# One 384-column projection from unshifted tokens, with V moved by 64 rows by DMA

## The chip, the cores and the metric

The kernel runs on one core of one Trainium2 chip. The metric is the device time of one launch in microseconds (us). Times shown are medians of several runs, each of the whole kernel. Names of engines in the profile: PE is TensorE's matmul, PEld its weight load, DVE is VectorE, ACT is ScalarE, POOL is GpSimd, SP is SyncE, which in this kernel issues nearly all DMAs.

## The reference

One encoder block on x of shape (1, 2048, 1024). The input is normalized, projected, and goes through two attention mixers: A with a window of 128 and grouped keys, B with three groups of eight heads whose windows and dilations are (128, 1), (512, 4) and (2048, 16). Their gated outputs are merged, projected and added to x.

```python
h = rms_norm(x, norm_gain[layer])
proj = h @ w_in[layer]
qa, ka, va, qb, kb, vb, ga, gb, mg = jnp.split(proj, split_idx, axis=-1)
...
for g, (window, dilation) in enumerate(B_GROUPS):
    o, l = dilated_group(qb[:, :, g], kb[:, :, g], vb[:, :, g], window, dilation,
                         rel_bias[:, c0:c0 + B_HEADS_PER_GROUP])
...
alpha = jax.nn.softmax(jnp.stack(lses, axis=0), axis=0)
yb = jnp.sum(alpha[..., None].astype(x.dtype) * jnp.stack(outs, axis=0), axis=0)
yb = yb.reshape(bsz, S, B_WIDTH) * jax.nn.silu(gb)
...
x = x + merged @ w_out[layer]
```

For dilation d, the tokens of one residue class (every d-th token) form a sequence of their own of 2048 / d tokens, and each of its tokens sees the 64 neighbours on either side. Queries and keys are normalized per head, with a bias by distance.

## The kernel before

**Operands.** x is normalized, scaled and split into two half-precision parts, XH (the rounded value) and XL (the rest), kept on chip for the whole main phase as 8 chunks of 128 channels by 2048 tokens, with 256 columns behind them (SE = 2048 + 256). Weights are split the same way into wh and wl. A product in nearly full precision is three matmuls: XH by wh, XH by wl, XL by wh.

**Units.** The main phase runs over 14 units (list UNITS): two units of A (four query heads, one key head, one value head each) and twelve of B (head pair p from 0 to 3, group g from 0 to 2; two query, two key, two value heads). Each unit has 384 weight columns: for B 128 of queries, 128 of keys, 128 of values. A unit goes through the 2048 tokens in 16 blocks of 128 tokens of one residue class, named (r, c): class r, block c. A class has n blocks: 16 in group 0, 4 in group 1, 1 in group 2.

**Slots.** The planner runs over slots, one per pair of blocks, 8 per unit, 112 in all. In a slot the matmuls of the pair's projections are written into TensorE's stream one by one, and all other steps are put in a queue of due times (functions `at` and `until`) measured in slots, and written out when TensorE's stream has come to that place. Each engine works in the order in which its instructions were written out. The constants EVAC, NORM, LS, LAGS and LV are these due times.

**Projection.** `Pair.matmuls` writes 24 matmuls (8 channel chunks by 3 operand pairs) into one PSUM bank "pj" (two banks). The tokens are the stationary operand, the weights the moving one, so that the result has tokens on partitions. In A and in group 2, one matmul makes all 384 columns. In groups 0 and 1 (`un.shift`), the query columns are made from the block's own 128 tokens, and the key and value columns from 128 tokens that lie 64 earlier (`subset(..., aligned=False)`), in a second series of 24 matmuls. So a query block i needs the keys and values of just the two shifted blocks i and i + 1. The first shifted block wraps: it has the last 64 tokens of the sequence and the first 64, and for that GpSimd copies the first 256 tokens behind XH and XL (`x_again`).

**After a pair's projection.** ScalarE copies queries and keys out of PSUM (`evac_qk`) and V's rounded part (`v_hi`), VectorE makes V's rest (`v_lo`); V goes into a tile "vt" (10 buffers) or "vw" for the wrapped first block (4 buffers), beside a column with a constant for the softmax denominator. Then come square, statistics, a reciprocal square root on GpSimd, scaling, gain, the split into two parts, and `turn`: SP issues DMA transposes that put heads on partitions (tile "kq", 4 buffers; one per block in B, and one for both blocks in A). Within a block's part of kq, queries and keys follow one another, each 128 tokens wide. The wrapped first block of group 0 gets a tile of its own (kq0), since the last query block reads it too.

**Items.** An `Item` is a query block with two heads. `logits` multiplies queries and keys into PSUM (one key range per matmul; two neighbouring whole blocks of one pair as one of 256 columns through `un.both`), `maxima` adds the bias and takes row maxima on VectorE, `exps`, `hi` and `lo` make the probabilities in two parts, `turn` lets SP transpose them (tile "pt"), and `values` multiplies them by V, LV slots after the start of the item. Where an item has fewer keys than its blocks are wide, `room` fills the rest of the row with zeros, so the value products always use whole blocks of 128 rows.

**SP's queue** carries weight loads, key transposes, transposes of probabilities, stores and loads of the B groups' partial results ("zd"), and stores of sums of x for the last third ("sd"). It works through them in the order of their due times: what waits holds up what stands behind.

**Last third.** After the main phase the gates, branch projections and the output projection run. There `piece` makes weight sums, and uses the 256 columns behind XH and XL as the place from which it stores them (`place`, `store`).

Of the kernel before, what the change touches and what calls it, by code (L numbers as in the profile page):

```python
# [22 lines left out]
F16 = mybir.dt.float16  # L23
# [7 lines left out]
S = 2048  # L31
D = 1024
NT = S // 128
# [5 lines left out]
PSC = 2.0 ** 14  # L39
VSC = 2.0 ** -13  # L40
SX = 2.0 ** 9
SE = S + 256
NG = 12


# [63 lines left out]
X_GB = ((0, 1), (1, 4))  # L109
X_AG, H_AT = .9, (.1, .35)  # L110
XR_BUFS = 6
XT_BUFS = 2
KQ_BUFS = 4
VT_BUFS = 10
PT_BUFS = 4
N_BIAS_A = 384
N_BIAS_B = 256
# [2 lines left out]
def block_kernel(tc, x, xt, w_units, w_gate, w_mrg, w_out, w_bra, w_brk, gain, qkg, sink, bias_a, bias_b, b_merge, out):  # L120
# [29 lines left out]
    ones = cst.tile([128, 128], F32, name="ones")  # L150
    G.memset(ones[:], 1.0)

    XH = xp.tile([128, NCH, SE], F16, name="XH")
    XL = xp.tile([128, NCH, SE], F16, name="XL")
    gp2, gi2 = [], []

    def pow2(mx, name):
# [593 lines left out]
    class Unit:  # L751


        def __init__(self, u):
            self.kind, self.idx, self.g = UNITS[u]
            self.u = u
            assert ("w", u) in done
            self.wh, self.wl = wtiles[u][3:5]
            if self.kind == "A":
                self.nq, self.nk, self.nv = 4, 1, 1  # L760
                self.d, self.n = 1, NT
            else:
# [6 lines left out]
            self.both, self.apart = {}, set()  # L769
# [27 lines left out]
    def subset(X, g, r, c, aligned):  # L797
        o = 128 * c if aligned else (128 * c or S // DIL[g]) - 64
        return xclass((XH, XL)[X], g, r)[:, :, o:o + 128]

    class Pair:

# [6 lines left out]
        def matmuls(self, i):  # L809
            un, (r, c) = self.un, self.subsets[i]  # L810
            self.ps[i] = ps = pj_p.tile([128, 512], F32, name="pj")
            out = []
            for a, b, aligned in ((0, 128, True), (128, 384, False)) if un.shift else ((0, 384, True),):
                h, lo = subset(0, un.g, r, c, aligned), subset(1, un.g, r, c, aligned)
                k = 0
                for ch in range(NCH):
                    for lhs, rhs in ((h, un.wh), (h, un.wl), (lo, un.wh)):
                        out.append(lambda lhs=lhs, rhs=rhs, ch=ch, a=a, b=b, k=k: T.matmul(  # L818
                            ps[:, a:b], lhsT=lhs[:, ch, :], rhs=rhs[:, ch, a:b], start=(k == 0), stop=(k == 23)))
# [30 lines left out]

        def v_lo(self, i):
            vt, psv = self.vt[i]
            nv = self.un.nv
            V.scalar_tensor_tensor(vt[:, :nv, 66:130], psv, VSC, vt[:, :nv, 0:HD], OP.mult, OP.subtract)
            self.un.v[self.subsets[i]] = vt

        def square(self):
            n = 2 * self.nh * HD
# [41 lines left out]
                G.tensor_copy(sp[:, i, nh:, :, :], sp[:, i, nq:nh, ::-1, :])  # L900

        def turn(self):
            kq = wk.tile([128, 12, 128], F16, name="kq", bufs=KQ_BUFS)
            outs = [kq[:, 6 * i:6 * i + 6] for i in range(2)]
            if self.un.shift and self.un.n == NT and self.subsets[0][1] == 0:
                outs[0] = wk.tile([128, 6, 128], F16, name="kq0", bufs=1)[:]
                self.un.apart.add(self.subsets[0])
            if self.un.kind == "A":
                nc.sync.dma_start_transpose(out=kq[:], in_=self.sp[:].rearrange("p s a b c -> p (s a b c)"))
            for i, s in enumerate(self.subsets):  # L910
                if self.un.kind == "B":
                    nc.sync.dma_start_transpose(out=outs[i], in_=self.sp[:, i].rearrange("p a b c -> p (a b c)"))
                self.un.kq[s] = outs[i]
            if len({s[0] for s in self.subsets}) == 1 and self.subsets[0] not in self.un.apart:
                self.un.both[self.subsets[0]] = kq[:].rearrange("p (i a) b -> p a i b", i=2)


    class Item:
        def __init__(self, un, r, i, h0):
            self.un, self.r, self.i, self.h0 = un, r, i, h0  # L920
            n = un.n
            self.p0 = 0
            if un.kind == "A":
                cs = [c for c in (i - 1, i, i + 1) if 0 <= c < n]
                self.keys = [((0, c), 0, 128) for c in cs]
                self.b0 = 128 * (cs[0] - i + 1)
            elif n == 1:
# [31 lines left out]
        def logits(self):  # L959
            un = self.un  # L960
            q = un.kq[(self.r, self.i)]
            if un.kind == "A":
                self.sv = [s_p.tile([128, 512], F32, name="s")[:, :self.W] for _ in range(2)]
            else:
                t = s_p.tile([128, 512], F32, name="s")
                self.sv = [t[:, self.W * j:self.W * j + self.W] for j in range(2)]
            for j in range(2):
                h = self.h0 + j
                kh = 0 if un.kind == "A" else h
                o, keys = 0, list(self.keys)  # L970
                while keys:
                    s, k0, k1 = keys.pop(0)
                    kt, w = un.kq[s][:, :, k0:k1], k1 - k0
                    if w == 128 and s in un.both and keys and keys[0] == ((s[0], s[1] + 1), 0, 128):
                        keys.pop(0)
                        kt, w = un.both[s], 256
                    for v in range(2):
                        T.matmul(self.sv[j][:, o:o + w], lhsT=q[:, h, :],  # L978
                                 rhs=kt[:, un.nq + kh + v * un.nk], start=(v == 0), stop=(v == 1))
                    o += w  # L980
# [38 lines left out]
        def values(self):  # L1019
# [3 lines left out]
            for j in range(2):  # L1023
                vh = 0 if un.kind == "A" else j
                for k, (p, c0, w) in enumerate(((self.ph, 0, HD + 1), (self.ph, 66, HD), (self.pl, 0, HD + 1))):
                    for s, key in enumerate(self.segs):
                        T.matmul(self.po[:, j, :w], lhsT=p[:, n * j + s, :], rhs=un.v[key][:, vh, c0:c0 + w],  # L1027
                                 start=(k == 0 and s == 0), stop=(k == 2 and s == n - 1))

        def z_load(self):  # L1030
# [759 lines left out]
    def piece(n, due):  # L1790
# [20 lines left out]
            r.append(w_sums(*raw, lambda t: t[:], tile))  # L1811

        def place(x, i):
            return (XH, XL)[x][:, i, S:SE]

        def store(x, a, e):
            o = 512 * c + 256 * m
            d = (wbd[k, x].rearrange("p (i o) -> p i o", i=7)[:, a:e, o:o + 256] if j < 4
                 else wod[:, a:e, x, j - 4, 256 * m:256 * m + 256])
            nc.sync.dma_start(out=d, in_=(XH, XL)[x][:, a:e, S:SE])  # L1820

        def hi(i):
            A.activation(place(0, i), r[0][0][i], AF.Copy, scale=sc[:])
# [454 lines left out]
```

## Time and profile before

| | us |
|---|---|
| median of 3 runs | 1884.11 (1883.85 to 1885.31) |
| the profiled execution | 1884.2 |
| its span, first to last instruction | 1882.4 |
| TensorE busy, matmuls | 1865.5 |
| VectorE busy | 1485.5 |
| ScalarE busy | 1242.8 |
| GpSimd busy | 579.1 |

The main phase's projections run from 108.0 to 1201.9 us of the span; the last third follows. By line, 45% of the chain of waits that ended last are the projection matmuls of line 818. In a row of the profile, "x" gives a count, and a matmul's duration is from its issue to the modelled end of its last result; consecutive matmuls overlap, so that the distance between their starts, in the timeline, is what they cost when TensorE is the limit. "128x256" is the size of the result, 128 partitions by 256 columns; "<-wh,XL 128*128" names the two operands and the size of the stationary one.

### The profile page before, as it was taken

To read this page: it belongs to the slowest core of one execution; us is meant where nothing else is said; L and a number is where in the kernel's file an instruction comes from. 1 tells how busy PE (TensorE), PEld (TensorE's weight loads), DVE (VectorE), ACT (ScalarE), POOL (GpSimd) and SP (SyncE) were. 2 spreads that over 40 slices of the span, in tenths; PEclk is the share of its full clock that TensorE was granted. 3 is DMA by queue.
4 is the path that set the end of the run, shared out by engine and by line. 5 is a ranking of instruction groups with operands and counts; after the bars stand their busy time and mean duration, and the time that the engine had idled before them with its cause. 6 is when DMAs were issued, how large, how long until landed. Compare 5 with 4: busy or idle time off the path is not lost.

```text
span 1882.4 us, 50311 instructions
## 1 busy us (share of the span) xinstructions
PE 1865.5 (99%) x18802; PEld 1430.3 (76%) x18802; DVE 1485.5 (79%) x3806; ACT 1242.8 (66%) x3002; POOL 579.1 (31%) x1363
## 2 busy tenths in 40 slices
PE   8999999999999999999999999999999999999999
PEld 5457996788999899998999989744444446776775
DVE  6649967998788788878789888857788764977885
ACT  8538877987777777677777667647667865433441
POOL 0024343444355345544355443510000001232121
PEclk9999999999999999999999999999999999999999
DMA  9236979897797688886898867877779978854552
GB/s 360 101 101 142 180 167 168 164 204 167 143 182 162 143 171 165 178 164 147 171 168 157 164 134 149 159 238 262 213 235 266 275 226 286 274 163 121 147 147 71
DMA packets 650021, 340.33 MB, mean 181 GB/s; under 512 B 459952, under 2 KB 590896, under 8 KB 648368
## 3 DMA queue, kind: packets, MB, share of 16 engines
q1 hardware_dynamic: 649632, 336.86, 74.3%
q8 instruction: 147, 2.41, 0.6%
q14 instruction: 98, 0.80, 0.2%
q10 hardware_dynamic: 144, 0.26, 0.0%
HBM read 149.05 MB, written 77.86 MB: 121 GB/s over the span
## 4 chain that ended last, share of the span: by engine, by line
PE 94%; DMA 2%; ACT 1%; DVE 1%; issue 1%; POOL 0%; SPq 0%; DVEq 0%; ACTq 0%; POOLq 0%
PE pj L818 45%; PE fps L1726 16%; PE fps L2051 8%; PE fps L2136 8%; PE s L978 5%; PE pv L1027 5%; PE pj L373 2%; PE pj L314 2%; PE fps L314 1%; DMA pt<-p 1%; PE pt L1081 1%; DMA wraw<-in_w_units_dram 0%; DMA xq<-in_xt_dram 0%; DVE pr L993 0%; DMA gtd<-yo 0%
## 5 line engine op out<-in xcount | busy, mean ns | idle before, releaser
L818 PE MATMUL pj<-wl,XH 128*128 128x128 f16 (+2 forms) x2816 | 715.3, 268 | 0.0
L818 PE MATMUL pj<-wh,XL 128*128 128x128 f16 (+2 forms) x2816 | 711.5, 269 | 0.0
L818 PE MATMUL pj<-wh,XH 128*128 128x128 f16 (+2 forms) x2816 | 708.7, 268 | 0.0
L818 PEld LDWEIGHTS <-XH 128*128 128x128 f16 x5632 | 576.6, 112 | 55.0
L818 PEld LDWEIGHTS <-XL 128*128 128x128 f16 x2816 | 315.6, 112 | 24.2
L993 DVE CUSTOM_DVE_ANT_0 pr<-s,b,ubuf 128x256 f32<-128x256 f32 (+3 forms) x512 | 218.9, 465 | 41.0 <-PE s L978 38.1
L1010 DVE SCALAR_TENSOR_TENSOR p<-pr,p 128x512 f16<-128x512 f32 (+2 forms) x256 | 194.4, 759 | 53.2 <-ACT p L1006 49.5
L885 POOL TENSOR_TENSOR rw<-rw,g 128x128 f32<-128x128 f32 (+1 forms) x224 | 148.3, 682 | 192.5 <-DVE rw L878 178.8
L2061 POOL TENSOR_TENSOR g<-g,t 128x512 f32<-128x512 f32 x32 | 48.3, 1510 | 484.8 <-DVE t L1983 484.4
L1726 PEld LDWEIGHTS <-wh 128*128 128x128 f16 x952 | 93.1, 98 | 111.3 <-issue 1.3
L836 ACT ACTIVATE rw<-pj 128x256 f32<-128x256 f32 (+1 forms) x224 | 87.3, 390 | 131.6 <-PE pj L818 131.0
L900 POOL COPY spl<-spl 128x256 f16<-128x256 f16 (+1 forms) x224 | 97.7, 465 | 244.4 <-DVE spl L895 243.7
L1006 ACT ACTIVATE p<-pr 128x512 f16<-128x512 f32 (+2 forms) x256 | 157.6, 616 | 4.6 <-POOL zz L1135 0.4
L2051 PE MATMUL fps<-y,bigh 128*128 128x128 f16 x1792 | 153.4, 219 | 0.0
L2051 PE MATMUL fps<-y,bigl 128*128 128x128 f16 x896 | 151.7, 219 | 0.0
L978 PE MATMUL s<-kq 128*128 128x128 f16 (+2 forms) x1552 | 149.3, 232 | 1.0 <-DVE nmA L993 0.9
L2136 PE MATMUL fps<-WO,mf 128*128 128x512 f16 x660 | 147.5, 379 | 0.0
L2051 PEld LDWEIGHTS <-bigh 128*128 128x128 f16 x1792 | 139.0, 98 | 7.3
L978 PEld LDWEIGHTS <-kq 128*128 128x128 f16 x1584 | 118.0, 98 | 19.8 <-issue 1.8
L1027 PE MATMUL pv<-vt,pt 128*128 128x65 f16 (+1 forms) x2784 | 131.6, 193 | 0.8 <-DMA pt<-p 0.7
L1027 PEld LDWEIGHTS <-pt 128*128 128x128 f16 x3024 | 120.0, 97 | 14.8 <-DMA pt<-p 1.8
L891 ACT ACTIVATE spl<-rw 128x512 f16<-128x512 f32 (+1 forms) x112 | 72.1, 643 | 76.5 <-POOL vt L847 70.1
(282 smaller groups left out, 3767.2 us busy)
## 6 DMA issues: line engine op xcount, KB each, us to landing
wraw<-in_w_units_dram SPq DMA_DIRECT2D x56, 384.0 KB, 4.0
g<-mgd SPq DMA_DIRECT2D x64, 256.0 KB, 5.2
mgd<-t SPq DMA_DIRECT2D x43, 256.0 KB, 4.5
wraw<-in_w_mrg_dram SPq DMA_DIRECT2D x41, 256.0 KB, 5.1
zd<-z SPq DMA_DIRECT2D x128, 66.0 KB, 2.1
zz<-zd SPq DMA_DIRECT2D x64, 132.0 KB, 3.5
ytd<-yo SPq DMA_DIRECT2D x32, 256.0 KB, 3.6
sd<-so SPq DMA_DIRECT2D x32, 256.0 KB, 2.8
```

The lines of the kernel that those rows point to most:

```text
L818: out.append(lambda lhs=lhs, rhs=rhs, ch=ch, a=a, b=b, k=k: T.matmul(ps[:, a:b], lhsT=lhs[:, ch, :], rhs=rhs[:, ch, a:b], start=(k == 0), ...
L836: A.activation(self.rw[:, n * i:n * i + n], self.ps[i][:, :n], AF.Copy)
L885: G.tensor_tensor(q[:, i, :un.nq, :], q[:, i, :un.nq, :], g, OP.mult)
L900: G.tensor_copy(sp[:, i, nh:, :, :], sp[:, i, nq:nh, ::-1, :])
L978: T.matmul(self.sv[j][:, o:o + w], lhsT=q[:, h, :], rhs=kt[:, un.nq + kh + v * un.nk], start=(v == 0), stop=(v == 1))
L993: V.tensor_tensor_reduce(out=self.pv[:, j, self.p0:self.p0 + W], in0=self.sv[j], in1=un.bias[:, self.h0 + j, self.b0:self.b0 + W], scale=I ...
L1006: A.activation(self.sp[:, :128 * n], self.pr, AF.Copy, scale=PSC)
L1010: V.scalar_tensor_tensor(self.sp[:, 128 * n:], self.pr, PSC, self.sp[:, :128 * n], OP.mult, OP.subtract)
L1027: T.matmul(self.po[:, j, :w], lhsT=p[:, n * j + s, :], rhs=un.v[key][:, vh, c0:c0 + w], start=(k == 0 and s == 0), stop=(k == 2 and s == n ...
L1726: T.matmul(b[k][:], lhsT=w[:, i, ch, :], rhs=xform(PROD[i][0], lo, ch, q), start=(i < 3 and n == 0), stop=(n == 11), skip_group_check=True)
L2051: out.append(lambda p=p, c=c, wl=wl, yl=yl, n=n: T.matmul(ps[:, 128 * p:128 * p + 128], lhsT=w[wl][:, i, c, p, :], rhs=y[:, yl, c, :], sta ...
L2136: out.append(lambda p=p, ml=ml, wl=wl, k=k: T.matmul(ps[:], lhsT=m[:, ml, p, :], rhs=WO[:, i, wl, p, :], start=(fresh and k == 0), stop=(k ...
```

## The change

All units now project all 384 columns in one series of 24 matmuls from unshifted tokens. Nothing is copied behind XH and XL any more, and these have 2048 columns.

Keys stay in unshifted blocks. In B the two blocks of a pair are now laid out in kq such that each head's keys of the pair are 256 tokens in a row; a query block's key range (64 before to 64 after it) is cut at multiples of 256, so it is one range of 192 at an end, or two of 192 and 64 columns. The transposes stay one per block, and write blocks of 128 at a distance of 256. Group 0 has no key tile of its own for the first block.

V of all units lies in one ring "vr" of 20 places in place of the tiles vt and vw. Where nothing is shifted, V is written there directly. In groups 0 and 1 it is written to a tile "vs" (one per pair, 2 buffers), and SP moves it into the ring by DMA, shifted by 64 rows (`v_move`, due 0.68 slots after the pair's projection): the first half of block c into the second half of place c, the second half into the first half of place c + 1. A class with n blocks takes n + 1 places; the first place has only its second half, the last one only its first half, and the value products of the query blocks at the ends use only those 64 rows of the stationary and the moving operand.

The pieces of the last third are stored from two tiles of their own.

```diff
-EVAC = (0.015, 0.025, 0.11)
+EVAC = (0.015, 0.025, 0.11, 0.68)
...
-VT_BUFS = 10
+V_RING = 20
...
-    def x_again(t, X):
-        G.tensor_copy(X[:, :, S + 128 * t:S + 128 * t + 128], X[:, :, 128 * t:128 * t + 128])
...
+    def subset(X, g, r, c):
+        return xclass((XH, XL)[X], g, r)[:, :, 128 * c:128 * c + 128]
+
+    vr = wk.tile([128, V_RING, 2, 130], F16, name="vr", bufs=1)
+    vpos = [0]
+
+    def v_place(n):
+        vpos[0] += n
+        return [k % V_RING for k in range(vpos[0] - n, vpos[0])]
...
-            for a, b, aligned in ((0, 128, True), (128, 384, False)) if un.shift else ((0, 384, True),):
-                h, lo = subset(0, un.g, r, c, aligned), subset(1, un.g, r, c, aligned)
-                k = 0
-                for ch in range(NCH):
-                    for lhs, rhs in ((h, un.wh), (h, un.wl), (lo, un.wh)):
-                        out.append(lambda lhs=lhs, rhs=rhs, ch=ch, a=a, b=b, k=k: T.matmul(
-                            ps[:, a:b], lhsT=lhs[:, ch, :], rhs=rhs[:, ch, a:b], start=(k == 0), stop=(k == 23)))
-                        k += 1
+            h, lo = subset(0, un.g, r, c), subset(1, un.g, r, c)
+            for ch in range(NCH):
+                for lhs, rhs in ((h, un.wh), (h, un.wl), (lo, un.wh)):
+                    k = len(out)
+                    out.append(lambda lhs=lhs, rhs=rhs, ch=ch, k=k: T.matmul(
+                        ps[:, 0:384], lhsT=lhs[:, ch, :], rhs=rhs[:, ch, :], start=(k == 0), stop=(k == 23)))
...
+            at(e[1] + EVAC[3], self.v_move)
...
-            if un.shift and self.subsets[i][1] == 0:
-                vt = wk.tile([128, 2, 130], F16, name="vw", bufs=4)
+            if not un.shift:
+                un.v[self.subsets[i]] = k = v_place(1)[0]
+                vt = vr[:, k]
             else:
-                vt = wk.tile([128, 2, 130], F16, name="vt", bufs=VT_BUFS)
-            G.memset(vt[:, :nv, HD:HD + 1], 2.0 ** -14)
+                if i == 0:
+                    self.vs = wk.tile([128, 2, 2, 130], F16, name="vs")
+                vt = self.vs[:, i]
+            G.memset(vt[:, :nv, HD:HD + 2], 2.0 ** -14)
...
+        def v_move(self):
+            un = self.un
+            if not un.shift:
+                return
+            r, c = self.subsets[0]
+            if c == 0:
+                for k, p in enumerate(v_place(un.n + 1)):
+                    un.v[r, k] = p
+            for src, dst, k in (0, 64, c), (64, 0, c + 1):
+                a, b = un.v[r, k], un.v[r, k + 1]
+                for i, p, n in ((0, a, 2),) if b == a + 1 else ((0, a, 1), (1, b, 1)):
+                    nc.sync.dma_start(out=vr[dst:dst + 64, p:p + n], in_=self.vs[src:src + 64, i:i + n])
...
+            by = kq[:].rearrange("p (a i) b -> p a i b", i=2)
             for i, s in enumerate(self.subsets):
-                if self.un.kind == "B":
-                    nc.sync.dma_start_transpose(out=outs[i], in_=self.sp[:, i].rearrange("p a b c -> p (a b c)"))
-                self.un.kq[s] = outs[i]
+                nc.sync.dma_start_transpose(out=by[:, :, i, :], in_=self.sp[:, i].rearrange("p a b c -> p (a b c)"))
+                un.kq[s] = by[:, :, i, :]
+                un.both[s] = kq[:].rearrange("p (a i) b -> p a (i b)", i=2), 128 * i
...
-                cs = [i, (i + 1) % n]
-                self.keys = [((r, i), 0 if i else 64, 128), ((r, (i + 1) % n), 0, 128 if i + 1 < n else 64)]
+                cs = [i, i + 1]
+                lo, hi = max(0, 128 * i - 64), min(128 * n, 128 * i + 192)
+                self.keys = [((r, k // 128), max(lo - k, 0), min(hi - k, 256)) for k in range(lo // 256 * 256, hi, 256)]
...
-                        T.matmul(self.po[:, j, :w], lhsT=p[:, n * j + s, :], rhs=un.v[key][:, vh, c0:c0 + w],
+                        a, b = (64 if un.shift and key[1] == 0 else 0), (64 if un.shift and key[1] == un.n else 128)
+                        T.matmul(self.po[:, j, :w], lhsT=p[a:b, n * j + s, :], rhs=vr[a:b, un.v[key], vh, c0:c0 + w],
                                  start=(k == 0 and s == 0), stop=(k == 2 and s == n - 1))
...
-    for k in range(4):
-        at(X_AG + .5 * k, x_again, k // 2, (XH, XL)[k % 2])
...
+    parts = [t3p.tile([128, 7, 256], F16, name=f"part{k}", bufs=1) for k in "hl"]
...
-            return (XH, XL)[x][:, i, S:SE]
+            return parts[x][:, i, :]
```

More of the change, by code (lines that the diff above doesn't have):

```diff
@@ L41 @@
 SX = 2.0 ** 9
-SE = S + 256
 NG = 12
@@ L109 @@
 X_GB = ((0, 1), (1, 4))
-X_AG, H_AT = .9, (.1, .35)
+H_AT = (.1, .35)
 XR_BUFS = 6
@@ L151, in block_kernel @@
     G.memset(ones[:], 1.0)
-    XH = xp.tile([128, NCH, SE], F16, name="XH")
-    XL = xp.tile([128, NCH, SE], F16, name="XL")
+    XH = xp.tile([128, NCH, S], F16, name="XH")
+    XL = xp.tile([128, NCH, S], F16, name="XL")
     gp2, gi2 = [], []
@@ L768, in __init__ @@
             self.v, self.kq, self.t, self.done = {}, {}, {}, {}
-            self.both, self.apart = {}, set()
+            self.both = {}
             if self.kind == "A" or self.g == 0:
@@ L854, in v_lo @@
             V.scalar_tensor_tensor(vt[:, :nv, 66:130], psv, VSC, vt[:, :nv, 0:HD], OP.mult, OP.subtract)
-            self.un.v[self.subsets[i]] = vt
+        def v_move(self):
[10 more added lines that the diff above has]
+                    nc.sync.dma_start(out=vr[dst:dst + 64, p:p + n], in_=self.vs[src:src + 64, i:i + n])
         def square(self):
@@ L902, in turn @@
         def turn(self):
+            un = self.un
             kq = wk.tile([128, 12, 128], F16, name="kq", bufs=KQ_BUFS)
[L904 to L908, printed above, removed]
-                nc.sync.dma_start_transpose(out=kq[:], in_=self.sp[:].rearrange("p s a b c -> p (s a b c)"))
-            for i, s in enumerate(self.subsets):
-                if self.un.kind == "B":
-                    nc.sync.dma_start_transpose(out=outs[i], in_=self.sp[:, i].rearrange("p a b c -> p (a b c)"))
-                self.un.kq[s] = outs[i]
-            if len({s[0] for s in self.subsets}) == 1 and self.subsets[0] not in self.un.apart:
-                self.un.both[self.subsets[0]] = kq[:].rearrange("p (i a) b -> p a i b", i=2)
+            if un.kind == "A":
+                nc.sync.dma_start_transpose(out=kq[:], in_=self.sp[:].rearrange("p s a b c -> p (s a b c)"))
+                for i, s in enumerate(self.subsets):
+                    un.kq[s] = kq[:, 6 * i:6 * i + 6]
+                un.both[self.subsets[0]] = kq[:].rearrange("p (i a) b -> p a i b", i=2)
+                return
+            by = kq[:].rearrange("p (a i) b -> p a i b", i=2)
+            for i, s in enumerate(self.subsets):
+                nc.sync.dma_start_transpose(out=by[:, :, i, :], in_=self.sp[:, i].rearrange("p a b c -> p (a b c)"))
+                un.kq[s] = by[:, :, i, :]
+                un.both[s] = kq[:].rearrange("p (a i) b -> p a (i b)", i=2), 128 * i
     class Item:
@@ L972, in logits @@
                     s, k0, k1 = keys.pop(0)
-                    kt, w = un.kq[s][:, :, k0:k1], k1 - k0
-                    if w == 128 and s in un.both and keys and keys[0] == ((s[0], s[1] + 1), 0, 128):
+                    w = k1 - k0
+                    if un.kind == "B":
+                        kt, k = un.both[s]
+                        kt = kt[:, :, k + k0:k + k1]
+                    elif s in un.both and keys and keys[0][0] == (s[0], s[1] + 1):
                         keys.pop(0)
                         kt, w = un.both[s], 256
+                    else:
+                        kt = un.kq[s]
                     for v in range(2):
@@ L1819, in store @@
                  else wod[:, a:e, x, j - 4, 256 * m:256 * m + 256])
-            nc.sync.dma_start(out=d, in_=(XH, XL)[x][:, a:e, S:SE])
+            nc.sync.dma_start(out=d, in_=parts[x][:, a:e, :])
         def hi(i):
```

3 lines of the change are left out of this document (removed).

## The prediction

> **What bounds the kernel now.** I read the page's first parts, then the windows of one stage, then TensorE's timeline.
>
> ```profile
> span 1882.4 us, 50311 instructions
> PE 1865.5 (99%) x18802; PEld 1430.3 (76%) x18802; DVE 1485.5 (79%) x3806; ACT 1242.8 (66%) x3002; POOL 579.1 (31%) x1363
> PE 94%; DMA 2%; ACT 1%; DVE 1%; issue 1%; POOL 0%; SPq 0%; DVEq 0%; ACTq 0%; POOLq 0%
> ```
>
> TensorE (PE) is busy for 99% of the span, and the chain of waits that ended last runs through it for 94%. A busy PE need not be full, since the ends of its matmuls are modelled, so I look at one stage, the group-0 unit of head pair 2, by the windows (busy us and instructions of PE, PEld, DVE, ACT, POOL; clock; DMA share; GB/s):
>
> ```profile
> 905.00:979.00 74.00, 74.00 (x1003) 69.38 (x1001) 60.16 (x183) 52.52 (x149) 32.19 (x90) 1.00 0.85 162
> ```
>
> PE has no gap there at a granted clock of 1.00, the other engines have 14 us or more to spare, and the 16 DMA engines are 85% busy. That last number is the one to keep in mind. So the time of this stage is the sum of what PE's instructions take from start to start, as long as nothing that feeds PE comes late.
>
> **What the change takes from PE.** The counts, by form (only one of the three operand pairs; the other two have the same counts):
>
> ```profile
> L818 PE MATMUL pj<-wh,XL 128*128 128x256 f16 x1024 | 279.2, 273 | 0.0
> L818 PE MATMUL pj<-wh,XL 128*128 128x384 f16 x768 | 253.4, 330 | 0.0
> L818 PE MATMUL pj<-wh,XL 128*128 128x128 f16 x1024 | 185.6, 219 | 0.0
> ```
>
> Three operand pairs make 3072 products of 128 columns and 3072 of 256 in the eight shifted units (groups 0 and 1), and 2304 of 384 in the other six. After the change the shifted units have 3072 of 384 instead: the same columns, 3072 matmuls and 3072 weight loads fewer. The durations 219, 273 and 330 ns overlap, so I take the distance between starts, from the timeline (start, modelled us) of a shifted stretch:
>
> ```profile
> 599.94 0.22 PE L818 MATMUL pj<-wh,XH 128*128 128x128 f16 x1
> ...
> 601.17 0.19 PE L1027 MATMUL pv<-vw,pt 128*128 128x65 f16 x1
> ...
> 601.64 0.27 PE L818 MATMUL pj<-wh,XH 128*128 128x256 f16 x1
> ...
> 603.28 0.50 PE L978 MATMUL s<-kq 128*128 128x64 f16 x8
> ...
> 605.83 0.52 PE L1027 MATMUL pv<-vt,pt 128*128 128x65 f16 x12
> 606.19 0.22 PE L818 MATMUL pj<-wl,XH 128*128 128x128 f16 x1
> ```
>
> From 599.94 to 601.17 stand 22 products of 128 columns: 1.23 / 22 = 0.0559 us each. From 601.64 to 603.28 stand 15 of 256: 0.1093 us each. The chain of waits in order of time has the 384-column ones, with nothing between:
>
> ```profile
> 108.14 22.75 PE pj L818 x140
> ```
>
> 22.75 / 140 = 0.1625 us each. One 128 and one 256 take 0.1652, so each replaced couple saves 0.0027 us; the starts are rounded to 0.01 us, which makes that 0.0027 +- 0.0009. Sum: 3072 x 0.0027 = **8.3 us** (5.5 to 11). It is a fixed cost of each matmul that goes, not arithmetic. PE is the path here, so it counts in full.
>
> A second term is the weight load, which is hidden behind the running matmul. By line, PEld at L818 in three windows (min/median/max ns), of the second A unit, of a group-1 unit and of a group-2 unit, and what stands behind it on PE:
>
> ```profile
> L818 PEld LDWEIGHTS <-XH x168: 95/98/181, 300.6 to 359.3; 128*128 128x128 f16 x168
> L818 PEld LDWEIGHTS <-XH x458: 111/113/181, 200.4 to 279.9; 128*128 128x128 f16 x153
> L818 PEld LDWEIGHTS <-XH x169: 142/144/207, 379.9 to 439.8; 128*128 128x128 f16 x169
> 611.52 0.36 PE L818 MATMUL pj<-wh,XL 128*128 128x384 f16 x1
> 611.72 0.33 PE L818 MATMUL pj<-wh,XH 128*128 128x384 f16 x1
> ```
>
> The load takes 98 ns from tokens side by side, 113 ns from every 4th, 144 ns from every 16th. In group 2 the first product after a block of values costs 0.20 us instead of 0.1625. If group 1 (113 ns) caught that too, its 64 items would lose 64 x 0.0375 = 2.4 us; if it behaves as the adjacent load, nothing. 113 is nearer to 98, so I take nothing and keep 2.4 us for the range.
>
> **What it moves on PE at little cost.** The logits (L978) keep their columns. Cutting the keys at pairs of blocks makes 120 matmuls of a group-0 unit's 100 and 96 of a group-1 unit's 112: 16 more in all, at 0.0027 us each nothing. The value products (L1027) keep their number, but those on a sequence's open end now use 64 of the 128 rows. Before, these are exactly the ones that read the wrap tile "vw":
>
> ```profile
> L1027 PE MATMUL pv<-vw,pt 128*128 128x65 f16 x160 | 19.8, 194 | 0.0
> L1027 PE MATMUL pv<-vw,pt 128*128 128x64 f16 x80 | 14.9, 191 | 0.0
> ```
>
> 240 matmuls of 40 items, each followed or preceded by a full one: 12 changes between half and full rows per item, 480 in all. The trace has no matmul of fewer than 128 rows. From below, such a change costs nothing, or gains nothing either, since a start-to-start distance goes by the columns. From above, each matmul waits until the one before has ended: 0.193 us of modelled duration instead of the 0.36 / 12 = 0.030 us that the block at 605.83 shows, 0.163 us more, 480 x 0.163 = 78 us. The nearest row is that block itself, with a different weight tile for each of its twelve, at 0.030; I take **zero** and keep the other end as a rival.
>
> **What it adds beside PE.** V no longer comes shifted from PE, so each of the 64 shifted pairs moves it by 64 rows with 2 DMAs (3 or 4 where the ring wraps) on SP's queue. The instruction rows and DMA issues of the stage above (line, count, KB, us to landing), and one slot of SP's and PE's timeline:
>
> ```profile
> L912 SPq DMA_TRANSPOSE kq<-spl x16: 1209/1242/2214, 908.7 to 973.5; - x16
> DMA to landing us min/median/max: 2.5/3.1/5.2
> L1062 SPq DMA_DIRECT2D zd<-z x11: 324/535/1288, 905.1 to 948.9; - x11
> wraw<-in_w_units_dram SPq DMA_DIRECT2D x4, 384.0 KB, 3.7
> sd<-so SPq DMA_DIRECT2D x4, 256.0 KB, 2.6
> wraw<-in_w_out_dram SPq DMA_DIRECT2D x4, 256.0 KB, 3.4
> zz<-zd SPq DMA_DIRECT2D x6, 132.0 KB, 3.5
> zd<-z SPq DMA_DIRECT2D x11, 66.0 KB, 2.1
> b<-in_bias_b_dram SPq DMA_DIRECT2D x2, 256.0 KB, 3.2
> pt<-p SPq DMA_TRANSPOSE x17, 3.8
> kq<-spl SPq DMA_TRANSPOSE x16, 3.1
> 942.01 2.74 SPq L912 DMA_TRANSPOSE kq<-spl  x2
> 948.54 0.61 PE L978 MATMUL s<-kq 128*128 128x128 f16 x8
> ```
>
> SP issues 33 transposes at 1.242 us and 31 plain DMAs at 0.535: 41.0 + 16.6 = 57.6 of 74 us. The change adds 17 at 0.535 = 9.1 us: 66.7 of the 72.9 us that PE would leave (74.0 less 8.3 / 8). It fits, with a tenth to spare. Queued behind a V move stand the transposes of probabilities and, half a slot later, those of the next keys. The keys are the tight ones: the second of the two at 942.01 starts at 943.38, lands 3.1 us later at 946.5, and the logits start at 948.54: 2.0 us of cover, against 1.07 us for two moves in front. The move itself waits for the V split of its pair, planned 0.57 slots (5 us) earlier, so it holds the queue for nothing. Its bytes (2 x 64 rows x 1040 B = 133 KB a slot) are what the zz load has, which lands in 3.5 us, and the values come over two slots later. Their load on the DMA engines is small too: 8 slots x 133 KB is 9% on the stage's 11.98 MB, so the share goes from 0.85 to at most 0.93. **Cost taken: zero**; without the cover each late slot costs up to 1.07 us.
>
> The keys' transposes of B now write blocks of 128 at a distance of 256. No row has that form; between an unchanged 3.1 us and 2.0 us more it is covered, so I take zero. The Trainium skill ("DMA: Bandwidth & Descriptors", Latency and other measured facts) gives DMA transposes some 30% less bandwidth when a middle dimension isn't contiguous; by it, as an estimate, 3.1 us would become 4.0, the cover would shrink to 1.1, and the second rival would gain. No run here shows it yet. The four POOL copies of X's first rows go from an engine that is 31% busy, the wrap's own key tile goes, the weight pieces of the last third write to a tile of their own with the same instructions: zero each.
>
> **Forecast.** The profiled execution took 1884.2 us (span 1882.4 and 1.8 around it), the median shown is 1884.11, so a sum against the one holds for the other. 1884.2 - 8.3 = **1876 us**, 0.4% less. A measurement of this kernel can tell about 0.2%, 3.8 us, from no change.
>
> **Rivals.**
> First, slower: **half rows make PE stop**. PE runs blocks of value products by overlapping about six of them (0.193 over 0.030). If a change between half and full rows ends that overlap, each of the 480 changes costs up to 0.163 us. It decides from 8.3 / 480 = 0.017 us a change. At half the bound, 0.08 us, it gives 1876 + 39 = 1915 us; at the full bound 1954. For it: nothing in this trace shows a half-row matmul running in such a stream. Against it: the overlap survives a new weight tile each time. The Trainium skill ("TensorEngine Tiling (Array Packing)", Tiling Modes, Key Properties) says that changing the tiling mode drains TensorE; by that rule, if 64 rows count as another mode, it is this rival that comes true.
>
> Second, no change: **SP's queue becomes the bound**. The two transposes at 942.01 take 1.37 us each, a tenth over the median. With every issue stretched by that tenth, SP needs 73.4 us of PE's 72.9; stretched by 15% (more DMA traffic, share above 0.9) 76.7, 3.8 us too many, of which the keys' cover takes 2.0 once: 1.8 x 4 group-0 units = 7 us, 1883 us. Against it: SP is idle for about 16 us of the 74 and group-2 units, which have no moves, let it catch up.
>
> Third, less than hoped: the couples save 0.0018 and group 1 pays its 2.4 us: 3.1 us, 1881. That is the low end of my own sum.
>
> **Chances.** Forecast 0.52 (1873 to 1880.4); the second and third together 0.13 (1880.4 to 1888); the first 0.35, because the rows exclude neither end of its price and the nearest one speaks for the lower; of that, 0.2 lies below 1915. With 0.15 left above, the range is **1873 to 1915**; the forecast's own is 1873 to 1880. Faster by over 0.2% 0.52, within 0.2% 0.13, slower 0.35.
>
> **What would show it.** Right: 5376 projections, all of 384 columns, 0.1625 us apart in groups 0 and 1 too; each shifted unit 1 us shorter; no PE idle before L978 from kq; half-row value products 0.03 us apart. The first rival would show blocks of twelve value products at an open end of 0.36 us grown to 1 us or more. The second would show key transposes issued later and logits waiting for them, with SP without a gap in group-0 units. Wrong altogether would be a wait of ACT or POOL for the two "vs" buffers or for a ring place.

## The result, and the profile after

After the change the kernel takes **1936.58 us** (median of 6 runs, 1935.98 to 1938.29), beside 1884.78 for the kernel before on the same chip: a ratio of 1.0276, 95% interval 1.0263 to 1.0289. It is 52 us slower, where 8 us faster was forecast.

From the page of the kernel after: span, busy time of each engine, and the chain that ended last by engine.

```profile
span 1934.2 us, 44444 instructions
...
PE 1910.4 (99%) x15746; PEld 1292.2 (67%) x15746; DVE 1488.6 (77%) x3806; ACT 1247.9 (65%) x3002; POOL 575.1 (30%) x1359
...
PE 91%; DMA 4%; DVE 1%; ACT 1%; issue 1%; POOL 0%; SPq 0%; DVEq 0%; ACTq 0%; POOLq 0%
```

PE has 18802 - 15746 = 3056 matmuls fewer (3072 couples merged, 16 logits more), and is busy for 45 us more. The chain still runs through it, at 91% rather than 94%. So most of the loss, 45 of 52 us, is time in which PE counts as busy.

To place it, I cut the span at the first projection of each unit and read the windows (busy us and instructions of PE, PEld, DVE, ACT, POOL; clock; DMA share; GB/s). Four units of the kernel before: group 0 of head pair 2, groups 1 and 2 of head pair 3, and the first shifted unit of all (group 1 of head pair 0).

```profile
905.34:978.54 73.20, 73.20 (x992) 68.68 (x990) 59.36 (x179) 52.26 (x148) 32.19 (x90) 1.00 0.86 163
978.54:1056.13 77.59, 77.59 (x1088) 77.23 (x1087) 68.90 (x219) 54.67 (x151) 42.32 (x109) 1.00 0.80 158
1056.13:1128.86 72.73, 72.73 (x627) 64.07 (x626) 63.23 (x181) 51.89 (x147) 31.65 (x83) 1.00 0.75 155
192.21:282.62 90.41, 90.29 (x1338) 89.29 (x1337) 72.76 (x201) 72.60 (x183) 37.47 (x91) 1.00 0.85 175
```

The same four units of the kernel after:

```profile
943.71:1017.20 73.49, 73.49 (x621) 48.06 (x618) 59.43 (x177) 52.68 (x148) 32.56 (x90) 1.00 0.85 173
1017.20:1098.82 81.62, 81.62 (x700) 60.01 (x699) 69.54 (x221) 55.08 (x151) 42.62 (x109) 1.00 0.83 164
1098.82:1177.78 78.96, 78.96 (x622) 67.43 (x621) 63.96 (x183) 51.99 (x147) 31.31 (x83) 1.00 0.66 144
192.17:293.18 101.01, 95.56 (x941) 71.42 (x940) 71.83 (x197) 72.33 (x183) 36.34 (x91) 0.98 0.88 165
```

Group 0 is 0.3 us longer, group 1 4.0 us, and group 2, whose projections the change does not touch, 6.2 us, all without a gap on PE. Only the first shifted unit has gaps (5.5 us), at a clock of 0.98. What a group-2 unit has is value products of the group-1 unit ahead of it, whose items end some slots after their projections: that is where to look. PE's timeline of the kernel after, in the first shifted unit (start, modelled us, then idle time before and who ended it):

```profile
251.22 0.53 PE L1051 MATMUL pv<-vr,pt 128*128 128x65 f16 x12 [3.26 <-DMA pt<-p]
251.59 0.33 PE L819 MATMUL pj<-wh,XL 128*128 128x384 f16 x1
...
251.97 0.53 PE L819 MATMUL pj<-wl,XH 128*128 128x384 f16 x1
252.29 0.53 PE L819 MATMUL pj<-wh,XL 128*128 128x384 f16 x1
...
262.11 0.33 PE L819 MATMUL pj<-wl,XH 128*128 128x384 f16 x1
262.37 1.68 PE L1051 MATMUL pv<-vr,pt 64*128 64x65 f16 x12
263.88 0.33 PE L819 MATMUL pj<-wh,XL 128*128 128x384 f16 x1
```

Two blocks of twelve value products. The one at 251.22, all of full rows, takes 0.37 us up to the next projection, much as before the change (0.36). The one at 262.37, in which half and full rows alternate, takes 1.51 us, and the projection ahead of it 0.26 instead of 0.1625. Beside the 0.36, that is 1.25 us more for 12 changes of rows: 0.104 us each. The page counts the whole block as busy, so no idle time points to it.

### The profile page after: what moved, and what is told of

Read it like the earlier page. It is cut to its first block, busy times and chain, and to the rows that moved or that the text cites. A ratio compares the mean times of both kernels' runs of the same rounds, so it can differ in the third digit from the quotient of the medians.

```text
span 1934.2 us, 44444 instructions
## 1 busy us (share of the span) xinstructions
PE 1910.4 (99%) x15746; PEld 1292.2 (67%) x15746; DVE 1488.6 (77%) x3806; ACT 1247.9 (65%) x3002; POOL 575.1 (30%) x1359
## 4 chain that ended last, share of the span: by engine, by line
PE 91%; DMA 4%; DVE 1%; ACT 1%; issue 1%; POOL 0%; SPq 0%; DVEq 0%; ACTq 0%; POOLq 0%
PE pj L819 43%; PE fps L1750 15%; PE fps L2075 8%; PE fps L2160 7%; PE pv L1051 7%; PE s L1001 5%; PE pj L372 2%; DMA pt<-p 2%; PE pj L313 1%; PE fps L313 1%; PE pt L1105 1%; DMA bigl<-sd 1%; DMA kq<-spl 1%; DMA wraw<-in_w_units_dram 0%; DMA xq<-in_xt_dram 0%
## 5 line engine op out<-in xcount | busy, mean ns | idle before, releaser
L819 PE MATMUL pj<-wh,XL 128*128 128x384 f16 x1792 | 588.2, 328 | 0.0
L819 PE MATMUL pj<-wl,XH 128*128 128x384 f16 x1792 | 584.7, 326 | 0.0
L819 PE MATMUL pj<-wh,XH 128*128 128x384 f16 x1792 | 584.6, 326 | 0.0
L819 PEld LDWEIGHTS <-XH 128*128 128x128 f16 x3584 | 416.0, 116 | 143.5 <-issue 0.7
L819 PEld LDWEIGHTS <-XL 128*128 128x128 f16 x1792 | 206.9, 115 | 62.1 <-issue 0.2
L1051 PEld LDWEIGHTS <-pt 128*128 128x128 f16 (+1 forms) x3024 | 150.2, 97 | 60.8 <-DMA pt<-p 9.3
L1051 PE MATMUL pv<-vr,pt 128*128 128x65 f16 (+2 forms) x3024 | 178.7, 194 | 6.1 <-DMA pt<-p 6.0
L1001 PE MATMUL s<-kq 128*128 128x128 f16 (+3 forms) x1600 | 150.8, 231 | 2.2 <-DMA kq<-spl 1.1
```

The lines of the kernel that those rows point to most:

```text
L819: out.append(lambda lhs=lhs, rhs=rhs, ch=ch, k=k: T.matmul(ps[:, 0:384], lhsT=lhs[:, ch, :], rhs=rhs[:, ch, :], start=(k == 0), stop=(k == ...
L1001: T.matmul(self.sv[j][:, o:o + w], lhsT=q[:, h, :], rhs=kt[:, un.nq + kh + v * un.nk], start=(v == 0), stop=(v == 1))
L1051: T.matmul(self.po[:, j, :w], lhsT=p[a:b, n * j + s, :], rhs=vr[a:b, un.v[key], vh, c0:c0 + w], start=(k == 0 and s == 0), stop=(k == 2 an ...
```

## Experiments

Theory: the 480 changes between half and full rows cost about 0.104 us each, 50 us, and the rest of the change behaves as forecast. Rivals: the loss comes from the V moves on SP's queue, or from the new place of V.

**1. Full rows.** Everything of the change stays but the half rows: the end blocks read all 128 rows of their ring place, and the rows that are no part of the sequence meet zeros in the probabilities.

```diff
+    G.memset(vr[:, :, 1], 0.0)
+    G.memset(vr[:, 16:20, 0], 0.0)
...
-                        a, b = (64 if un.shift and key[1] == 0 else 0), (64 if un.shift and key[1] == un.n else 128)
+                        a, b = 0, 128
```

> The changed kernel, but the value products at a sequence's ends use all 128 rows of a ring place again (the half that was never moved in holds old or zero values, and meets zeros in the probabilities). Theory 1, a price per change between half and full rows (a block of twelve takes 1.51 us plus 0.10 before it in place of 0.36, 40 blocks, 50 us): about 1886 us, blocks back at 0.36. Theory 2, the V moves on SP's queue and the DMA engines cost most of it: stays above 1925.

Measured: 1890.67 us (ratio to before 1.0029, 1.0018 to 1.0040). 46 us of the 52 are gone. Of the 134 blocks of twelve value products that stand in one piece, 39 took 1.51 to 1.60 us in the kernel after; here all take some 0.36 us, but for one of 0.65 behind a wait, shown in experiment 4. It is still 6 us slower than before, not 8 faster; experiment 4 takes that up.

**2. Fewer changes.** The same products in another order: head 0 does its three full ones first and then its three halves, head 1 the other way round. 240 half-row products stay, with 2 changes in an item rather than 12.

```diff
-                        T.matmul(self.po[:, j, :w], lhsT=p[a:b, n * j + s, :], rhs=vr[a:b, un.v[key], vh, c0:c0 + w],
-                                 start=(k == 0 and s == 0), stop=(k == 2 and s == n - 1))
+                        todo.append((b - a, p, c0, w, s, key, a, b))
+                todo.sort(key=lambda e: e[0] if j else -e[0])
+                for k, (_, p, c0, w, s, key, a, b) in enumerate(todo):
+                    T.matmul(self.po[:, j, :w], lhsT=p[a:b, n * j + s, :], rhs=vr[a:b, un.v[key], vh, c0:c0 + w],
+                             start=(k == 0), stop=(k == len(todo) - 1))
```

> The changed kernel with the same 240 half-row value products, but within an item in the order full, full, full, half, half, half for the first head and half, half, half, full, full, full for the second: 2 changes of row count per item in place of 12, 80 in all in place of 480. If each change costs 0.104 us: 1936.6 - 400 x 0.104 = 1895 us. If each half-row matmul costs 0.21 us wherever it stands: no difference, 1936.

Measured: 1896.17 us (1.0059, 1.0044 to 1.0074). PE's timeline of one such block, which carries six halves in its middle:

```profile
645.73 0.33 PE L819 MATMUL pj<-wl,XH 128*128 128x384 f16 x1
645.89 0.73 PE L1055 MATMUL pv<-vr,pt 128*128 128x65 f16 x12
646.47 0.36 PE L819 MATMUL pj<-wh,XL 128*128 128x384 f16 x1
```

0.58 us, 0.22 over an all-full block, for two changes: 0.11 each. (80 of them make 8.8 us; this median and that of experiment 1 are 5.5 apart. In the profiled executions this kernel waited less in its first shifted unit, which took 95 us rather than 97.) So six half rows one after another add nothing that can be seen beside the two changes; it is the change that costs.

**3. Half rows alone, in the kernel before.** Only the 240 products that read "vw" get 64 rows.

```diff
-                        T.matmul(self.po[:, j, :w], lhsT=p[:, n * j + s, :], rhs=un.v[key][:, vh, c0:c0 + w],
+                        e0, e1 = (64 if un.shift and self.i == 0 and s == 0 else 0), (64 if un.shift and self.i == un.n - 1 and s == 1 else 128)
+                        T.matmul(self.po[:, j, :w], lhsT=p[e0:e1, n * j + s, :], rhs=un.v[key][e0:e1, vh, c0:c0 + w],
```

> The kernel before with one thing alone: the 240 value products that read the wrap tile use only the 64 rows that count. No V moves, no ring, no 384-column products in groups 0 and 1. Theory 1: 1884.8 + 50 = 1935 us. Theory 2 (V moves): 1885 us.

Measured: 1935.22 us (1.0266, 1.0251 to 1.0282), 50.5 us more than before, or 0.105 for each of the 480 changes. It has no ring, no V moves and no new projections, so the rival causes are out for these 50 us. Here the trace has the products one by one; PE's timeline:

```profile
292.63 0.20 PE L1028 MATMUL pv<-vw,pt 64*128 64x65 f16 x1
292.77 0.20 PE L1028 MATMUL pv<-vt,pt 128*128 128x64 f16 x1
292.90 0.20 PE L1028 MATMUL pv<-vw,pt 64*128 64x64 f16 x1
...
293.98 0.20 PE L1028 MATMUL pv<-vw,pt 64*128 64x65 f16 x1
```

From 292.63 to 293.98 are ten changes: 0.135 us from start to start, where a block of full rows has 0.030. The modelled duration rose only from 0.19 to 0.20: start-to-start distances show this cost, durations don't.

The weight loads say more. PEld's timeline of the block at 605.83 in the kernel before (first line, from the start of its first load to the end of its last), and of the block above (the other two):

```profile
605.78 0.45 PEld L1027 LDWEIGHTS <-pt 128*128 128x128 f16 x12
...
292.35 0.10 PEld L1028 LDWEIGHTS <-pt 128*128 128x128 f16 x1
292.63 1.44 PEld L1028 LDWEIGHTS <-pt 64*128 64x128 f16 x11 [0.18 <-issue]
```

Among full rows a product's weights are loaded ahead of it: the load at 605.78 is for the product at 605.83, the one at 292.35 for the product at 292.51. The load for the first half-row product starts at 292.63, with the product itself, after PEld has stood idle for 0.18 us. So at a change of rows the next weights are not loaded ahead; whether that is the cause of the price or goes with it, no run here separates. By unit the price is the same: experiment 3 lengthens a group-0 unit, with one such item, by 1.25 us, a group-1 unit, with four, by 5.04, and a group-2 unit, with five from the unit ahead, by 6.3.

**4. The V moves on ACT's queue.** Experiment 1 with one word changed.

```diff
-                    nc.sync.dma_start(out=vr[dst:dst + 64, p:p + n], in_=self.vs[src:src + 64, i:i + n])
+                    nc.scalar.dma_start(out=vr[dst:dst + 64, p:p + n], in_=self.vs[src:src + 64, i:i + n])
```

> As e1_full_rows, and the V moves are issued from ScalarE's queue in place of SP's. If what is left over in e1_full_rows is SP's queue (the 3.3 us wait for pt at 251 us in the first shifted unit and the slower clock after it): about 7 us less than e1_full_rows, 1879 us, and no such wait. If it is the DMA engines or something else: the same as e1_full_rows, or more if ScalarE's issuing delays its evacuations.

Measured: 1878.72 us (1877.82 to 1881.01; ratio 0.9968, 0.9957 to 0.9980). It is 12 us faster than experiment 1, and **faster than both kernels**: than the one before by 6.0 us, 0.3%. The same four units as above:

```profile
903.04:975.25 72.21, 72.21 (x621) 47.42 (x619) 59.27 (x177) 52.19 (x148) 32.42 (x90) 1.00 0.87 178
975.25:1051.83 76.58, 76.58 (x699) 57.40 (x698) 69.28 (x221) 54.80 (x151) 42.77 (x109) 1.00 0.89 171
1051.83:1124.49 72.66, 72.66 (x622) 64.02 (x620) 63.42 (x183) 52.00 (x148) 31.91 (x83) 1.00 0.77 159
191.38:284.17 92.79, 89.76 (x941) 68.98 (x940) 72.82 (x199) 72.29 (x183) 36.84 (x91) 1.00 1.00 180
```

Groups 0 and 1 are 0.99 and 1.01 us shorter than before, group 2 is as before. Only the first shifted unit is 2.4 us longer, with 3 us of gaps on PE and the DMA engines at a share of 1.00. In experiment 1 it was 97.29 us; that unit, and the group-0 unit of head pair 2:

```profile
194.49:291.78 97.29, 92.53 (x943) 70.13 (x940) 71.86 (x197) 72.46 (x183) 36.41 (x91) 0.96 0.87 171
913.75:985.95 72.20, 72.20 (x619) 47.43 (x618) 59.35 (x177) 52.67 (x148) 32.22 (x90) 1.00 0.83 176
```

So the queue's 4.5 us in the first shifted unit are 1.7 us more of gaps, and 2.8 us in which PE is busy for longer, at a clock of 0.96. SP's own timeline there shows where the gaps come from (start, us of issuing, DMA):

```profile
244.90 0.43 SPq L188 DMA_DIRECT2D wraw<-in_w_units_dram  x1
245.44 1.23 SPq L1041 DMA_TRANSPOSE pt<-p  x1
246.72 0.58 SPq L188 DMA_DIRECT2D wraw<-in_w_units_dram  x1
247.34 1.13 SPq L874 DMA_DIRECT2D vr<-vs  x2
248.58 1.63 SPq L1041 DMA_TRANSPOSE pt<-p  x1
```

SP goes from one issue to the next: the transposes of probabilities stand behind weight loads and two V moves. PE's timeline there has the value products that wait for them:

```profile
252.55 0.84 PE L1053 MATMUL pv<-vr,pt 128*128 128x65 f16 x12 [3.49 <-DMA pt<-p]
```

PE's waits in the whole of experiment 1 (us in total, times, longest):

```profile
PE pv L1053 <- DMA pt<-p: 5.6, 5, 3.5
...
PE s L1003 <- DMA kq<-spl: 3.4, 5, 1.5
```

And in experiment 4:

```profile
PE pv L1053 <- DMA pt<-p: 3.3, 3, 1.9
...
PE s L1003 <- DMA kq<-spl: 0.3, 1, 0.3
```

By the starts of the units, 8.1 us of the difference between the two profiled executions (spans of 1890.9 and 1876.8; that of experiment 1 was the slowest of its eight) lie within the units: 4.5 in the first shifted one, 1.8 and 0.9 in the group-1 and group-0 units of head pair 1, where PE waits for keys. 2.9 us lie ahead of the first unit, where there are no V moves yet, and about 3 behind the last; these I don't ascribe to the queue. The chain of waits in order of time has the same 25 matmuls there, first in experiment 1, then in experiment 4:

```profile
63.29 7.08 PE pj L372 x25
62.03 5.40 PE pj L372 x25
```

1.7 of the 2.9 us are these: in experiment 1 the granted clock is 0.54 from 63.3 to 66.7 us, in experiment 4 it is 1.00 there.

**5. Moves later.** Experiment 1 with the moves due 1.27 slots after the projection rather than 0.68, to test whether the place in SP's queue matters rather than the number of moves.

```diff
-EVAC = (0.015, 0.025, 0.11, 0.68)
+EVAC = (0.015, 0.025, 0.11, 1.27)
```

> As e1_full_rows (moves on SP), but the V moves are due 1.27 slots after the projection, just behind the key transposes, in place of 0.68. If it is their place in SP's queue that costs (they hold up the keys and probabilities queued behind them): most of the 12 us between e1 and e4 comes back, about 1880 us. If it is their number on a queue that has little time to spare: 1887 us or more, since they now hold up the probabilities instead, and the two vs buffers come free later.

Measured: 1989.02 us (1.0552, 1.0537 to 1.0568). The second theory had no upper end and named the "vs" buffers, but 98 us over experiment 1 is far beyond what either had in view. Its waits:

```profile
ACT vs L854 <- DMA vr<-vs: 176.8, 53, 6.0
...
DVE vs L860 <- ACT vs L854: 148.0, 56, 4.8
...
POOL vs L853 <- DMA vr<-vs: 139.9, 54, 5.4
...
PE pj L821 <- DVE vs L860: 50.8, 35, 2.7
```

This answers another question: the two "vs" buffers. A move that leaves 0.59 slots later holds its buffer when the next pair's V wants it; ACT and POOL wait, then DVE, then PE for the PSUM bank. These 51 us of PE's are about half of the loss; PE is also busy for 22 us longer (1885.4 against 1863.6), at a mean granted clock of 0.991 rather than 0.997. In the kernel after, POOL waits for a "vs" buffer once, for 3.2 us. So the question of place against number stays open; what is shown is that the moves have little room to be late.

**6 and 7. Moves twice, on SP and on ACT.** Experiments 1 and 4 with every move issued a second time into a tile "vx" that nobody reads (shown for SP; for ACT the copy is on nc.scalar).

```diff
+            vx = wk.tile([128, 2, 2, 130], F16, name="vx")
...
+                    nc.sync.dma_start(out=vx[dst:dst + 64, i:i + n], in_=self.vs[src:src + 64, i:i + n])
```

> As e1_full_rows, with every V move issued a second time on SP's queue, into a tile that nothing reads. In group-0 units of the changed kernel SP is issuing for 68 to 71 of 73.5 us; 17 more at 0.6 us make 78 to 81. If SP's issuing is the limit: 5 to 9 us more in each of the four group-0 units and some in the first group-1 unit, 1915 to 1930 us. If it is not: 1891 to 1895.

> As e4_full_rows_act_queue, with every V move issued a second time on ScalarE's queue: the same extra bytes as e6_double_moves_sp without a single issue on SP. If the DMA engines' load is what the moves cost: as far above 1878.7 as e6 is above 1890.7. If SP's issuing is it: 1879 to 1886, with the difference in the first shifted unit, where the engines are 96% busy already in the kernel before.

Measured: 1962.81 us on SP (1.0415, 1.0387 to 1.0444), 72 more than experiment 1; 1918.32 on ACT (1.0178, 1.0162 to 1.0193), 40 more than experiment 4. On SP, from the waits and the windows (the group-0 unit of head pair 2):

```profile
PE s L1005 <- DMA kq<-spl: 59.3, 32, 5.0
```

```profile
954.12:1035.20 81.08, 74.36 (x620) 48.05 (x618) 59.25 (x179) 53.00 (x148) 31.93 (x90) 0.98 0.80 165
```

That is the second rival, made large: SP's issues in that unit add up to 74.1 us, more than the 72.2 that PE needs, the logits wait for their keys, and a unit takes 81 us, as expected. The whole was 33 us above the upper end of what was expected, which counted the four group-0 units and some of the first group-1 unit. But group-1 units have as many moves and took 5.7 to 8.6 us more than in experiment 1 (the first of all 1.7), and group-2 units of head pairs 1 to 3, which have moves only of the unit ahead, 4.3 to 7.9 us more. On ACT I had expected almost nothing, and that fell:

```profile
ACT p L1033 <- issue: 51.5, 27, 3.4
...
ACT p L1033 <- DMA vx<-vs: 24.3, 8, 4.0
...
PE s L1005 <- DMA kq<-spl: 13.5, 13, 3.4
```

ACT's exponentials ("p") stood behind its own DMA issues; in experiment 4 the first of these rows has 7.3 us, 6 times, and the second doesn't exist. ACT's queue is therefore not free room, only room enough for one set of moves. The copies also double the moves' bytes and have a buffer of their own to wait for, so how much of the 40 us is issuing, how much DMA traffic and how much that buffer isn't settled.

**8. Earlier weights.** Experiment 4 still has waits for "pt" in the first shifted unit, where SP also loads the weights of the third unit. Here these are loaded in the unit before.

```diff
-W_LOAD = (0.1, 0.75), (0.6, 0.25)
+W_LOAD = (0.1, 0.75), (-3.7, 0.35)
```

> As e4_full_rows_act_queue, but the weights of the third unit (4 x 384 KB, until now loaded at about 230 to 245 us, in the crowded first shifted unit) are loaded in the unit before, where the DMA engines are 64% busy. If the 3.2 us of waiting for pt at 242 to 250 us and the slower clock behind it come from full DMA engines: about 1875 us, and no such wait. If not: 1878 to 1880.

Measured: 1879.57 us (0.9971, 0.9960 to 0.9982), the same as experiment 4. Its first two units, by the windows:

```profile
110.15:196.66 86.51, 83.50 (x789) 56.65 (x788) 67.03 (x181) 62.41 (x142) 28.88 (x72) 1.00 0.71 143
196.66:286.23 89.57, 89.31 (x942) 69.13 (x940) 72.30 (x196) 72.33 (x184) 35.93 (x89) 1.00 0.97 173
```

The first shifted unit went from 92.79 to 89.57 us and PE's gaps there shrank from 3.0 to 0.3 us, as expected. But the unit ahead went from 84.48 to 86.51, and the start of the span was 3.2 us longer in this execution. Of the 3.2 us gained, 2.0 are lost again one unit earlier, where the weights are now loaded. The longer start is much the one of experiment 1: the 25 matmuls at 63.60 take 7.08 us, with a granted clock of 0.50 from 63.6 to 67.0. That is 1.7 us of the longer start, and nothing here ties it to the moved loads: this execution was the slowest of its eight.

## Why the prediction was wrong

**What bounds the kernel**: right. PE ran without a gap in the units shown but the first shifted one, and their times follow from PE's start-to-start distances alone.

**3072 couples, 8.3 us**: right. Per shifted unit that is 8.3 / 8 = 1.04; experiment 4 shows 0.99 and 1.01, with 384 columns still 0.1625 us apart (eight in a row from 905.01 to 906.31 in its group-0 unit). **Weight load of group 1, nothing**: right, since group 1 gains as much as group 0. The logits' 16 more matmuls are within these numbers.

**Half rows, zero**: this is the step that failed. The prediction took 0.030 us from "the nearest row", a full-row block with a new weight tile for each matmul. That row says that new weights don't end the overlap; it says nothing of a change of rows, and no other row of the trace did. The bound from above, 0.163, held: the price is 0.104 us, 480 x 0.104 = 50 us. So the first rival came true, in the place and the form it named (blocks of 0.36 us grown to 1.5 or 1.6). The prediction gave this rival a chance of 0.35, and 0.15 to a time above its range. The range missed it because it was cut at half the bound, 1915, and no row chose that half. The Trainium skill ("TensorEngine Tiling (Array Packing)", Key Properties) says that changing the tiling mode, not just the tile, drains TensorE. If 64 rows among 128 count as another mode, each change drains. The traces agree with that: 0.104 to 0.11 us a change, nothing to be seen for half rows in a row, and weights that are not loaded ahead at a change; that it is a drain, no row names.

**V moves on SP, zero**: too low, mostly in another place than the one argued. The sum of SP's issues was good: 67.0 us in the group-0 unit of head pair 2 of the kernel after, where 66.7 was forecast. It leaves out the 0.05 us or more between two issues (246.67 to 246.72 above), some 4 us for 81 of them as an estimate. In three of the four group-0 units the cover held: 72.20 us with SP (experiment 1) in that unit, 72.21 with ACT. The fourth lost 0.9 us. The first shifted unit, where SP also has 25 transposes of probabilities to issue rather than 17, and eight stores "ytd", was not looked at, and it lost 4.5 us to the queue. What came late there was "pt", not the keys. So the second rival had the mechanism and mostly the wrong unit; it priced 7 us, and experiments 1 and 4 are 12 us apart, of which 8.1 lie in units by their profiles. The Trainium skill ("DMA: Bandwidth & Descriptors", Issuing engines are not separate DMA queues) says that issuing from more engines saves only the sequencer's time, usually small beside the DMA. By size the traces agree: 0.59 us for a move beside 2.3 to landing (experiment 1's medians). But on one queue these times add up, with 1.2 to 1.6 us for a transpose, and PE waited for what stood behind them.

**Key transposes into strided blocks, zero**: right. SP's row and landing times in the group-0 unit of the kernel after:

```profile
L930 SPq DMA_TRANSPOSE kq<-spl x16: 1209/1238/2398, 946.0 to 1012.6; - x16
...
DMA to landing us min/median/max: 2.8/3.2/5.1
```

3.2 us against 3.1 before. The 4.0 us that the prediction worked out from the Trainium skill were not seen. (30% less bandwidth would make 3.1 / 0.7 = 4.4 us rather, as an estimate, if all of that time went by bandwidth.)

**Accounts.** 40 items x 1.25 us = 50 us of changes, 8 us of couples gained, and in the first shifted unit 101.01 - 90.41 = 10.6 us, of which 3 items are 3.75 and the couples -1, so some 8 us of waits and slower clock. 50 - 8 + 8 = 50 of the 51.8 us between the two spans. By unit, with one, four and five such items in a unit of group 0, 1 and 2: 1.25 - 1.04 = 0.2, 5.0 - 1.04 = 4.0 and 6.25 us, where the windows show 0.3, 4.0 and 6.2.

## What to carry to other kernels

In this kernel a matmul of 64 rows was no cheaper than one of 128, and changing between them cost: zero the rows that don't count and keep all of a stream at 128 rows, or group the short ones so that rows change seldom. When no row of a profile shows a property that the change introduces, the nearest row that varies something else is no price for it; take the bound itself into the range. A queue's room has to be added up in the unit where it does the most besides, not in the one that is easiest to read.

## What the runs showed of the hardware that was not expected

A change between 64 and 128 rows costs 0.104 to 0.11 us in either direction, while the profile counts it as busy time and lengthens the modelled duration by 0.01 us. At a change the next weights are not loaded ahead.

After PE's wait of 3.26 us in the kernel after, the projections stand 0.32 us apart (251.97, 252.29), twice 0.1625; the granted clock is 0.51 from 251.8 to 255.2 us. The waits of 1.9 us and less in the first shifted unit of experiment 4 have no such effect: the granted clock of that unit is 1.00. The Trainium skill ("TensorE: Matmul & The Clock Gate", What's actually happening) has the clock halved after an idle window of about 3.4 us; the waits of 3.26 us and, in experiment 1, 3.49 us are near that. They are not the whole of it: the lower clock at 63.3 us of experiment 1 stands behind two waits of only 0.80 and 1.85 us, and experiment 2, with 0.69 and 1.85 us there, kept 1.00. What decides there stays open.
